# Softmax over rows on one Trainium2 core: all transfers in SyncE's queue, and the scaling by one broadcasting multiplication per group on GpSimd and VectorE

## The chip, the cores and the metric

The kernel runs on one core of a Trainium2 chip. The core has VectorE (DVE in the profile), ScalarE (ACT), GpSimd (POOL), SyncE (SP), TensorE (PE, not used here) and 16 DMA engines between the main memory and the on-chip memory, whose 128 partitions each hold a row of the tile at work. The metric is the time of one execution on the device, in microseconds (us), as a median over runs.

## The reference

The input is 16 x 1024 rows of 512 float32 numbers; each row is turned into its softmax.

```python
def reference(x: np.ndarray) -> np.ndarray:   # x: (16, 1024, 512) float32
    x_max = np.max(x, axis=-1, keepdims=True)
    exp_x = np.exp(x - x_max)
    return (exp_x / np.sum(exp_x, axis=-1, keepdims=True)).astype(np.float32)
```

## The kernel before, in words

The 16,384 rows are cut into eight chunks of 2,048 rows. In a chunk every partition holds 16 consecutive rows, so that one chunk is one transfer of 4 MB, 32 KB for each partition. The tile `held` has six places for chunks; chunk k lies in place k modulo 6, and all the work is done in place: a row is loaded, overwritten by its exponentials, overwritten again by the scaled result, and stored from there. Chunks 6 and 7 go into places 0 and 1, so their loads have to wait until the stores of chunks 0 and 1 have landed.

A chunk is worked on in two groups of eight rows per partition (`GROUP`), which makes sixteen groups, numbered 0 to 15; groups 2k and 2k+1 belong to chunk k. Each group takes three steps:

- `rowmax(g)`, line 88: one VectorE instruction takes the negated maximum of each of the eight rows and writes them to `shift`.
- `exps(g)`, line 93: eight ScalarE instructions, one for each row, compute the exponentials with `shift` as the bias, and leave the row's sum in `sums`.
- `scale(g)`: a VectorE reciprocal of the eight sums (line 104, into `recip`) and then eight VectorE instructions (line 106), one for each row, that multiply the row by its reciprocal.

The schedule is written out by hand (`tc.manual_schedule`), and every engine takes its instructions in program order. The loop over the groups calls `rowmax(g)`, `exps(g)` and then `scale(g - 1)`, so VectorE does the maximum of a group before it scales the group in front.

The six loads at the start are issued from SyncE's queue (line 71), the first one ahead of the start barrier (`loads_at_the_head`). The eight stores are issued from ScalarE's queue (line 74), among its exponentials. `STORE_BEHIND` says how many groups later than the last group of its chunk a store is placed, and `LOAD_AFTER` places the loads of chunks 6 and 7 in SyncE's queue at the points of the program at which the stores of chunks 0 and 1 are placed in ScalarE's. The small tiles `shift`, `sums` and `recip` have six buffers each.

Of the kernel before, what the change touches and what calls it, by code (L numbers as in the profile page):

```python
# [1 line left out]

# [4 lines left out]

F32 = mybir.dt.float32
EXP = mybir.ActivationFunctionType.Exp
AX = mybir.AxisListType.X  # L10


CHUNK = 16
CHUNKS = 8
PLACES = 6
GROUP = 8

STORE_BEHIND = [1, 1, 1, 1, 0, 0, 0, 0]

LOAD_AFTER = {0: 6, 1: 7}  # L20


AT_HEAD = {mybir.EngineType.SP: 1}

def loads_at_the_head(nc):

    main, body = nc.main_func.blocks[0], nc.main_func.blocks[1]
    for engine, count in AT_HEAD.items():  # L30
        loads = [
            i
            for i in body.instructions
            if i.engine == engine and type(i).__name__ == "InstDMACopy"
        ][:count]
        barrier = next(
            n
            for n, i in enumerate(main.instructions)
            if i.engine == engine and type(i).__name__ == "InstDrain"
        )  # L40
        for load in loads:
            body.instructions.remove(load)
        main.instructions[barrier:barrier] = loads


@with_exitstack
def kernel(
    ctx: ExitStack,
    tc: tile.TileContext,
    x: bass.AP,  # L50
    out: bass.AP,
):
    nc = tc.nc
    nc.at_finalize(loads_at_the_head)
    P = nc.NUM_PARTITIONS

    x_rows = x.flatten_outer_dims().rearrange("(c p r) d -> c p r d", p=P, r=CHUNK)
    out_rows = out.flatten_outer_dims().rearrange("(c p r) d -> c p r d", p=P, r=CHUNK)
    n, _, _, d = x_rows.shape
    assert n == CHUNKS  # L60

    data = ctx.enter_context(tc.tile_pool(name="data", bufs=1))
    stats = ctx.enter_context(tc.tile_pool(name="stats", bufs=6))
    held = data.tile([P, PLACES * CHUNK, d], F32, name="held")

    def place(k):
        at = (k % PLACES) * CHUNK
        return held[:, at : at + CHUNK, :]

    def load(k):  # L70
        nc.sync.dma_start(out=place(k), in_=x_rows[k])  # L71

    def store(k):
        nc.scalar.dma_start(out=out_rows[k], in_=place(k))
        if k in LOAD_AFTER:
            load(LOAD_AFTER[k])

    per = CHUNK // GROUP
    groups = CHUNKS * per
    shift, sums = [None] * groups, [None] * groups  # L80

    def rows(g):
        at = (g % per) * GROUP
        return place(g // per)[:, at : at + GROUP, :]

    def rowmax(g):
        shift[g] = stats.tile([P, GROUP], F32, name="shift", tag="shift")
        nc.vector.reduce_max(out=shift[g], in_=rows(g), axis=AX, negate=True)  # L88

    def exps(g):  # L90
        sums[g] = stats.tile([P, GROUP], F32, name="sums", tag="sums")
        for r in range(GROUP):
            nc.scalar.activation(  # L93
                out=rows(g)[:, r, :],
                in_=rows(g)[:, r, :],
                func=EXP,
                bias=shift[g][:, r : r + 1],
                scale=1.0,
                accum_out=sums[g][:, r : r + 1],
            )  # L100

    def scale(g):
        recip = stats.tile([P, GROUP], F32, name="recip", tag="recip")
        nc.vector.reciprocal(out=recip, in_=sums[g])  # L104
        for r in range(GROUP):
            nc.vector.tensor_scalar_mul(  # L106
                out=rows(g)[:, r, :],
                in0=rows(g)[:, r, :],
                scalar1=recip[:, r : r + 1],
            )  # L110

    with tc.manual_schedule():
        for k in range(PLACES):
            load(k)
        stored = 0
        for g in range(groups):
            rowmax(g)
            exps(g)
            if g:
                scale(g - 1)  # L120
            if stored < CHUNKS and g > (stored + 1) * per - 1 + STORE_BEHIND[stored]:
                store(stored)
                stored += 1
        scale(groups - 1)
        while stored < CHUNKS:
            store(stored)
            stored += 1


# [1 line left out]
_INS = ['x']  # L131
_OUTS = [((16, 1024, 512), 'float32')]


# [23 lines left out]
```

## Time and profile before

| | |
|---|---|
| Median of 3 runs (lowest to highest) | 161.43 us (161.29 to 161.83) |
| The profiled execution: its own time, and its span | 161.69 us, 159.9 us |
| VectorE busy | 123.5 us, 77% of the span |
| ScalarE busy | 93.2 us, 58% of the span |
| GpSimd busy | 0.2 us |
| Read from and written to main memory | 33.55 MB each, 420 GB/s in the mean |
| Packets of the loads' and of the stores' DMA queue | 49.5% and 48.6% of the time of 16 DMA engines |

The profile is that of one execution. The span is the time from the first to the last instruction or transfer; the execution's own time is 1.8 us longer. The share of a DMA queue is the time that its packets took, over the time of all 16 engines. In a group of instructions "busy, mean ns of one" is the sum and the mean of the instructions' durations; successive instructions of VectorE or ScalarE can overlap by their ends, so the distance from one start to the next can be shorter than the mean.

### The profile page before, as it was taken

The numbers are of one execution on the slowest core, as the hardware profiler recorded it, in microseconds if no ns is written. First come the engines' busy times: TensorE is split into PE (matmuls) and PEld (weight loads), VectorE is DVE, ScalarE is ACT, GpSimd is POOL, SyncE is SP. The second block draws the span as 40 slices with busy tenths as digits, with TensorE's granted clock in tenths as the row PEclk, the third lists the DMA queues.
The fourth block names the chain that finished last, engine by engine and source line by source line (L and its number), as shares of the span: only waits on it lengthen the run. The fifth ranks groups of instructions, "written<-read, shape, count | busy, mean of one in ns | idle before, by whom it ended". The sixth has DMA issues, their size and how long they took to land.

```text
span 159.9 us, 496 instructions
## 1 busy us (share of the span) xinstructions
DVE 123.5 (77%) x160; ACT 93.2 (58%) x257; POOL 0.2 (0%) x4
## 2 busy tenths in 40 slices
DVE  0008969999999999999999999999999997620000
ACT  0003799495959585867777685959594959300000
POOL 0000000000000000000000000000000000000000
DMA  8999999999999999999999999999999999999993
GB/s 270 459 443 402 451 459 402 426 469 410 402 393 393 500 412 402 467 434 410 426 459 410 418 484 404 402 500 410 402 426 484 393 410 500 402 402 500 410 402 148
DMA packets 2307, 67.13 MB, mean 420 GB/s; under 512 B 256, under 2 KB 256, under 8 KB 256
## 3 DMA queue, kind: packets, MB, share of 16 engines
q1 hardware_dynamic: 1152, 33.55, 49.5%
q10 hardware_dynamic: 1152, 33.55, 48.6%
q14 instruction: 3, 0.02, 0.0%
HBM read 33.55 MB, written 33.55 MB: 420 GB/s over the span
## 4 chain that ended last, share of the span: by engine, by line
DMA 48%; DVE 32%; ACT 8%; issue 1%; DVEq 0%; SPq 0%; ACTq 0%
DMA held<-in_x_dram 30%; DVE shift L88 19%; DMA out_dram<-held 18%; DVE held L106 12%; ACT held L93 8%; DVE recip L104 1%; DVEq L153 0%; SPq L71 0%; ACTq L93 0%
## 5 line engine op out<-in xcount | busy, mean ns | idle before, releaser
L93 ACT ACTIVATE held<-held,shift 128x512 f32<-128x512 f32 x128 | 90.5, 708 | 31.5 <-DVE shift L88 21.3
L88 DVE TENSOR_REDUCE shift<-held 128x8 f32<-128x4096 f32 x16 | 70.5, 4415 | 12.7 <-DMA held<-in_x_dram 12.7
L106 DVE TENSOR_SCALAR held<-held,recip 128x512 f32<-128x512 f32 x128 | 52.1, 482 | 0.6
L93 ACT ACTIVATION_READ_ACCUMULATOR held<-held,shift 128x1 f32 x128 | 23.9, 187 | 0.0
L93 ACT ACT_TABLE_LOAD x1 | 1.3, 1283 | 12.6 <-DMA held<-in_x_dram 12.6
L104 DVE RECIPROCAL recip<-sums 128x8 f32<-128x8 f32 x16 | 3.1, 196 | 4.0 <-ACT held L93 4.0
L142 POOL MEMSET const-bfloat16-1.0<- 128x1 bf16 x1 | 0.1, 101 | 0.0
L142 POOL MEMSET const-uint8-127<- 128x1 uint8 x1 | 0.1, 101 | 0.0
L142 POOL MEMSET const-float32-0.0<- 128x1 f32 x1 | 0.1, 98 | 0.2 <-issue 0.2
L142 POOL MEMSET const-float32-1.0<- 128x1 f32 x1 | 0.1, 98 | 0.0
## 6 DMA issues: line engine op xcount, KB each, us to landing
held<-in_x_dram SPq DMA_DIRECT2D x8, 4096.0 KB, 35.4
out_dram<-held ACTq DMA_DIRECT2D x8, 4096.0 KB, 28.4
```

Source lines behind the costliest of these rows:

```text
L88: nc.vector.reduce_max(out=shift[g], in_=rows(g), axis=AX, negate=True)
L93: nc.scalar.activation(out=rows(g)[:, r, :], in_=rows(g)[:, r, :], func=EXP, bias=shift[g][:, r : r + 1], scale=1.0, accum_out=sums[g][:, ...
L104: nc.vector.reciprocal(out=recip, in_=sums[g])
L106: nc.vector.tensor_scalar_mul(out=rows(g)[:, r, :], in0=rows(g)[:, r, :], scalar1=recip[:, r : r + 1],)
L142: nc = _bacc.Bacc("TRN2", target_bir_lowering=False, num_devices=1)
```

## The change

All stores are issued from SyncE's queue as well, so the order of the sixteen transfers is that of one queue: loads 0 to 5, store 0, store 1, load 6, store 2, load 7, then stores 3 to 7. A store now stands directly behind the scaling of the second group of its chunk (`finish`), and `STORE_BEHIND` is gone.

The eight multiplications of a group become one instruction over 128 x 4096 numbers, whose second operand is `recip`, repeated along each row. For groups 0 to 11 GpSimd issues it, for groups 12 to 15 VectorE. The reciprocal stays on VectorE, as do the maxima.

```diff
-STORE_BEHIND = [1, 1, 1, 1, 0, 0, 0, 0]
+LOAD_BEHIND = {1: 6, 2: 7}

-LOAD_AFTER = {0: 6, 1: 7}
+ON_POOL = range(12)
...
     def store(k):
-        nc.scalar.dma_start(out=out_rows[k], in_=place(k))
-        if k in LOAD_AFTER:
-            load(LOAD_AFTER[k])
+        nc.sync.dma_start(out=out_rows[k], in_=place(k))
+        if k in LOAD_BEHIND:
+            load(LOAD_BEHIND[k])
...
     def scale(g):
         recip = stats.tile([P, GROUP], F32, name="recip", tag="recip")
         nc.vector.reciprocal(out=recip, in_=sums[g])
-        for r in range(GROUP):
-            nc.vector.tensor_scalar_mul(
-                out=rows(g)[:, r, :],
-                in0=rows(g)[:, r, :],
-                scalar1=recip[:, r : r + 1],
-            )
+        engine = nc.gpsimd if g in ON_POOL else nc.vector
+        engine.tensor_mul(
+            out=rows(g),
+            in0=rows(g),
+            in1=recip.unsqueeze(2).to_broadcast([P, GROUP, d]),
+        )
+
+    def finish(g):
+        scale(g)
+        if (g + 1) % per == 0:
+            store(g // per)
...
-        stored = 0
         for g in range(groups):
             rowmax(g)
             exps(g)
             if g:
-                scale(g - 1)
-            if stored < CHUNKS and g > (stored + 1) * per - 1 + STORE_BEHIND[stored]:
-                store(stored)
-                stored += 1
-        scale(groups - 1)
-        while stored < CHUNKS:
-            store(stored)
-            stored += 1
+                finish(g - 1)
+        finish(groups - 1)
```

## The prediction

> **What bounds the kernel now.** I read the page's head and its 40 slices first, then the DMA queues, the busy time by stage, the groups of instructions, and the timeline around the first scaling.
>
> ```profile
> span 159.9 us, 496 instructions
> DVE 123.5 (77%) x160; ACT 93.2 (58%) x257; POOL 0.2 (0%) x4
> DMA  8999999999999999999999999999999999999993
> q1 hardware_dynamic: 1152, 33.55, 49.5%
> q10 hardware_dynamic: 1152, 33.55, 48.6%
> ```
>
> The DMA engines are full from the first slice to the last, and the two queues share them half and half (q1 loads, q10 stores). No compute engine comes near. The stages say the same:
>
> ```profile
> 12.50:40.00 27.50, 25.90 (x27) 20.09 (x54) 0.00 (x0) 1.00 1.01 435
> 56.00:84.00 28.00, 27.89 (x34) 20.79 (x59) 0.00 (x0) 1.00 1.00 431
> 84.00:120.00 36.00, 35.62 (x51) 27.29 (x77) 0.00 (x0) 1.00 1.00 432
> 141.00:160.00 19.00, 0.00 (x0) 0.00 (x0) 0.00 (x0) 1.00 0.84 364
> ```
>
> The last two columns are the DMA share and the rate. Loads alone (12.5 to 40), both directions (56 to 120): 431 to 435 GB/s throughout. One queue fills the engines as well as two do, so the single queue by itself neither costs nor brings rate. The trace's records of single packets put the loads' landings at 12.5, 22.2, 31.9 and 41.6 us: 9.69 us for a transfer that has the engines to itself, and the last four stores are as far apart. The first packet starts 1.34 us after the first issue, the last ends at 159.1, 0.8 before the end of the span. So sixteen transfers end to end, the first landing at 12.5, would end at 12.5 + 15 x 9.69 = 157.9, the span at 158.7. Before is only 1.2 us above that. The gain has a floor at that; the loss has none.
>
> The time is the span plus 1.79 us for the profiled execution (161.69 - 159.9), and that execution lies 0.26 above the median of the runs; so I add 1.53 to a span. Full engines give 158.7 + 1.53 = 160.2.
>
> **The transfers.** In one queue the slots begin, if nothing is late: store 0 at 60.9, store 1 at 70.6, load 6 at 80.3 (landing 90.0), store 2 at 90.0, load 7 at 99.7 (landing 109.4), stores 3 to 7 at 109.4, 119.1, 128.8, 138.5 and 148.2. Load 6 waits in SyncE's queue until store 0 has landed (70.6), under cover of store 1's 9.69 us; load 7 waits for store 1 (80.3), under cover of load 6 and store 2. Behind each wait stand all later transfers: a store that isn't ready stops even those that are. That is the price of the fixed order. ScalarE is rid of eight issues of some 0.34 us and SyncE gets eight, with 9.7 us for each: nothing. A store's issue must come 1.34 us before its slot (the first load's latency). So group 5 must be scaled by 88.7, group 7 by 108.1, group 9 by 117.8, group 11 by 127.5.
>
> **The compute that stays.**
>
> ```profile
> L93 ACT ACTIVATE held<-held,shift 128x512 f32<-128x512 f32 x128 | 90.5, 708 | 31.5 <-DVE shift L88 21.3
> L88 DVE TENSOR_REDUCE shift<-held 128x8 f32<-128x4096 f32 x16 | 70.5, 4415 | 12.7 <-DMA held<-in_x_dram 12.7
> L106 DVE TENSOR_SCALAR held<-held,recip 128x512 f32<-128x512 f32 x128 | 52.1, 482 | 0.6
> L142 POOL MEMSET const-bfloat16-1.0<- 128x1 bf16 x1 | 0.1, 101 | 0.0
> ```
>
> ```profile
> 22.74 0.20 DVE L104 RECIPROCAL recip<-sums 128x8 f32<-128x8 f32 x1 [1.49 <-ACT held L93]
> 22.98 3.26 DVE L106 TENSOR_SCALAR held<-held,recip 128x512 f32<-128x512 f32 x8
> 26.15 4.42 DVE L88 TENSOR_REDUCE shift<-held 128x8 f32<-128x4096 f32 x1
> ```
>
> A group now costs VectorE 4.42 + 0.2 + 3.26 = 7.9 us in a row. The change takes 3.26 of that away for twelve groups, and ScalarE, which waited 21.3 us for `shift`, then sets the pace with 5.76 us for eight exponentials (16.96 to 22.71 in the chain of waits). Off the path: group 11 is exponentiated by 86, and its scaling is due at 127.5.
>
> **The multiplications on GpSimd.** Group 0 can start at 23.0, and twelve of them run one behind the other, since GpSimd will be slower than ScalarE's 5.76. The trace has nothing of GpSimd but fills of 0.1 us, so the price P of 128 x 4096 products is bounded by VectorE's rows. Below: 4.42, the maximum's pass over one operand of that size. Above: 13.2, three such passes one after the other (two operands read, one written). I take two passes, 8.83, because the instruction reads two operands and nothing shows that GpSimd can read them side by side. Without any disturbance group 9 is then done at 23.0 + 88.3 = 111.3, in time, and group 11 at 129.0, 1.5 us late. P = 8.70 would be just in time. At 13.2 group 11 is done at 181.4, and the time is 181.4 + 1.34 + 3 x 9.69 + 0.8 + 1.53 = 214.
>
> **The multiplications on VectorE.** Four passes of 128 x 4096; bounds 3.26 (the present eight instructions) and 8.83 (two passes); I take 4.42, one pass, as the maximum's row of the same size. Alone they are hidden: group 15 is scaled by about 133, and due at 146.9. But they run while GpSimd works off its backlog, on two operands each, as it does. What they cost each other lies between nothing and full exclusion. The row that bears on it is L106: 512 products start every 407 ns, while the maximum passes 512 numbers in 4415/8 = 552. VectorE thus reads one tensor faster than one stream does, so it has a second way into memory, which a second operand would use. Whether GpSimd uses that same way, no row shows. I take exclusion, instruction by instruction, as likelier, since it needs only that the second operand of the one and the operands of the other meet at that one way; no cost stays in the range.
>
> The Trainium skill ("SBUF — State Buffer", section "Who interferes with whom") speaks against the change here: a VectorE instruction with two operands in the on-chip memory and a GpSimd instruction that reads it exclude each other for a whole instruction, and VectorE's plain reduction excludes nobody. By that rule the time is the 174.9 below, without it 161.7; nothing of before shows it.
>
> The walk, with taking turns: maximum 12 from 90.0, exponentials to 100.2; VectorE asks for multiplication 12 at 100.5, gets it when GpSimd ends group 8 (102.5), to 106.9. GpSimd does group 9 to 115.7. Load 7 lands at 109.4, maximum 14 to 113.8, multiplication 13 asked for at 114.0, run 115.7 to 120.1. Group 10 to 128.9. Multiplication 14, asked for at 124.8, 128.9 to 133.3. Group 11 from 133.3 to 142.2. GpSimd loses three turns, 3 x 4.42 = 13.2. Store 5 starts at 143.5 instead of 128.8; with stores 6 and 7 behind it the last packet ends at 143.5 + 29.1 = 172.6, the span at 173.4, the time is 174.9.
>
> For P a page has a figure ("GPSIMD Engine Reference", section "Elementwise — side-by-side cycle accounting"): 4497 ns for 2048 float32 sums per partition. Doubled, an estimate of 8.99 us for ours; the same walk would give 176.8. No row here shows it.
>
> **The rivals.**
>
> Taking turns (forecast): 174.9. If GpSimd is never made to wait and VectorE is, multiplication 12 starts at 129.0, and VectorE's four multiplications and two maxima in a row, with exponentials 15 between, end at 157.2; store 7 then ends at 168.2 and the time is 170.5. Sharing in part lies between 162 and 175. For it: both engines read two operands, and GpSimd has work in every moment at which VectorE asks. Against it: no row.
>
> GpSimd late by itself, no disturbance: 158.7 + 1.5 + 1.53 = 161.7 at P = 8.83, 163.8 at P = 9.0, 160.2 at 8.70. Most of it is no change or a little slower.
>
> No stall at all, the faster side: the engines stay full, 160.2; and 160.9 if the slow packets that before has at 40 to 44 us, as its first store starts, come again (0.66 us). It decides at P = 8.70 without disturbance and at (127.5 - 23.0 - 13.2)/12 = 7.6 with three lost turns. For it: P could be as low as 4.42, and the disturbance unreal.
>
> GpSimd much slower, P over 9.2: upwards of 177 with taking turns, up to 214 without.
>
> That the change doesn't do what it says I give nothing: in the built program the sixteen transfers stand in SyncE's queue in the order named, and the twelve multiplications in GpSimd's.
>
> **How the numbers follow.** Exclusion in whole or in part 0.45; late without disturbance 0.22 (faster 0.02, no change 0.10, slower 0.10); no stall 0.24; much slower 0.09. A measurement of this kernel can tell a change from none at about 0.3%, 0.5 us. So faster 0.26, same 0.10, slower 0.64. The predicted time is the first case's, 174.9; its own range is 166 to 177. The range must reach down to the no-stall case and leaves out the much slower one: 160.0 to 177.0.
>
> **What would show it right or wrong.** Right: GpSimd's twelve multiplications end near 142, three of them or the gaps before them stretched by some 4.4 us in 100 to 135; the DMA row falls to zero from about 129 to 143; SyncE's longest wait stands before store 5. Wrong in price: a GpSimd row far from 8.8 us. Wrong in exclusion: VectorE's multiplications at 4.4 us beside an unbroken row of GpSimd's. Wrong altogether: a DMA row of nines to the end, a span of 158.7, and the last transfer store 7 at 148.2.

## The result and the profile after

The changed kernel takes 163.65 us (163.43 to 163.99), the kernel before 161.63 us in the same comparison: a ratio of 1.0119, 95% interval 1.0093 to 1.0145. It is slower, by 2.0 us, and not by the 13 that were forecast.

The first view is the head of the changed kernel's page: busy time of the engines, the 40 slices, the rate in each slice, and the DMA queues.

```profile
span 161.4 us, 412 instructions
DVE 92.7 (57%) x36; ACT 91.9 (57%) x257; POOL 83.9 (52%) x16
POOL 0000039999999999999999999940000000000000
DMA  7999999999999999999989999999999999999990
GB/s 268 487 414 398 487 414 398 489 406 406 487 406 406 479 292 463 439 390 471 439 384 479 431 390 471 439 390 463 447 390 463 447 390 463 447 390 463 447 390 16
q1 hardware_dynamic: 2304, 67.11, 97.4%
q14 instruction: 2, 0.02, 0.0%
```

The DMA row is full to the end: the hole that was forecast for 129 to 143 us isn't there. GpSimd is done by slice 27, at 106.5 us, 21 us before its last group was due. What has changed is the last slice. It is 4 us long and moves 16 GB/s, which is two packets of 32 KB; in the kernel before the last slice moved 148 GB/s. For its last two microseconds the span waits for one DMA engine of sixteen. Of the kernel before, the rates and the queue that the prediction does not show:

```profile
GB/s 270 459 443 402 451 459 402 426 469 410 402 393 393 500 412 402 467 434 410 426 459 410 418 484 404 402 500 410 402 426 484 393 410 500 402 402 500 410 402 148
q14 instruction: 3, 0.02, 0.0%
```

The groups of instructions, and VectorE's timeline where its first multiplication meets GpSimd's last:

```profile
L93 ACT ACTIVATE held<-held,shift 128x512 f32<-128x512 f32 x128 | 90.3, 707 | 27.1 <-DVE recip L104 24.0
L106 POOL TENSOR_TENSOR held<-held,recip 128x4096 f32<-128x4096 f32 x12 | 83.7, 7022 | 22.3 <-DVE recip L104 22.3
L88 DVE TENSOR_REDUCE shift<-held 128x8 f32<-128x4096 f32 x16 | 70.1, 4388 | 27.3 <-DMA held<-in_x_dram 27.3
L106 DVE TENSOR_TENSOR held<-held,recip 128x4096 f32<-128x4096 f32 x4 | 20.6, 5139 | 0.1
```

```profile
92.51 14.00 POOL L106 TENSOR_TENSOR held<-held,recip 128x4096 f32<-128x4096 f32 x2
...
103.51 7.28 DVE L106 TENSOR_TENSOR held<-held,recip 128x4096 f32<-128x4096 f32 x1
...
116.74 4.42 DVE L106 TENSOR_TENSOR held<-held,recip 128x4096 f32<-128x4096 f32 x1
```

GpSimd's multiplication takes 7.02 us, and twelve of them follow one another without a gap. VectorE's takes 4.42 alone, and 7.28 where it began at 103.51 beside GpSimd's last, which ended at 106.51: it waited the 3.0 us and then ran its own 4.3. GpSimd was not held up at all.

The last engine can be told from the records of single packets. Every transfer ends with one completion record from each of the sixteen DMA engines. The records don't name the engine; its packets were put together by their times, since each begins where the one before it ends. The times of packets given below are 0.34 us later than the records have them, so that they match the landings. The table says how far the last and the second-to-last completion lie behind the middle one, for the last store:

```
               middle ends at   second-to-last   last
kernel before      157.85           +1.18       +1.26 us
changed kernel     157.99           +0.33       +2.55 us
```

The sum's 157.9 for sixteen transfers in a row holds for the middle engine in both. By the records every engine moves eight of a transfer's 128 packets, 128 data packets of 1.213 us in all, one behind the other and without gaps. It is late only by what is put among its packets or lengthens them. On the late engine of the changed kernel there are two 8 KB packets of the queue called "instruction" (0.31 us each, and the data packet behind each is 0.25 to 0.32 longer), and three data packets of loads that are 0.3 to 0.8 longer, at 58.8, 60.8 and 90.0 us, each the last or the last but one packet of a load with a store behind it. At 58 to 60 every engine loses time in this way (0.92 us in the middle, 1.61 on this one); at 90 only this one does (0.34).

So of the 1.88 us between the two profiled executions (163.57 and 161.69), 1.3 is the last engine's delay (2.55 - 1.26), 0.15 the middle one's, and 0.4 lies outside the span (2.17 against 1.79).

### The profile page after: what moved, and what is told of

It reads as the page before. It is cut to its first block, busy times and chain, and to the rows that moved or that the text cites. A ratio compares the mean times of both kernels' runs of the same rounds, so it can differ in the third digit from the quotient of the medians.

```text
span 161.4 us, 412 instructions
## 1 busy us (share of the span) xinstructions
DVE 92.7 (57%) x36; ACT 91.9 (57%) x257; POOL 83.9 (52%) x16
## 4 chain that ended last, share of the span: by engine, by line
DMA 46%; POOL 14%; DVE 10%; issue 8%; ACT 7%; ACTq 0%; DVEq 0%
DMA held<-in_x_dram 26%; DMA out_dram<-held 20%; POOL held L106 14%; ACT held L93 7%; DVE held L106 5%; DVE shift L88 4%; DVE recip L104 1%; ACTq L151 0%; DVEq L104 0%
## 5 line engine op out<-in xcount | busy, mean ns | idle before, releaser
L106 POOL TENSOR_TENSOR held<-held,recip 128x4096 f32<-128x4096 f32 x12 | 83.7, 7022 | 22.3 <-DVE recip L104 22.3
L106 DVE TENSOR_TENSOR held<-held,recip 128x4096 f32<-128x4096 f32 x4 | 20.6, 5139 | 0.1
```

The lines of the kernel that those rows point to most:

```text
L106: engine.tensor_mul(out=rows(g), in0=rows(g), in1=recip.unsqueeze(2).to_broadcast([P, GROUP, d]),)
```

## The experiments

All ratios are to the kernel before, on the same chip. For the profiled execution of a run, "behind" is the distance of the last engine from the middle one. A "fetch" is an 8 KB packet of the queue called "instruction", a "ring" is what one queue has waiting at one DMA engine, and a "turn" is a place where the transfers change from a load to a store.

**The queue alone, and the scaling alone.**

```diff
# e1_queue_only, against the changed kernel
-        engine = nc.gpsimd if g in ON_POOL else nc.vector
-        engine.tensor_mul(out=rows(g), in0=rows(g), in1=...)
+        for r in range(GROUP):
+            nc.vector.tensor_scalar_mul(...)        # as before
# e2_scale_only, against the kernel before
-        for r in range(GROUP):
-            nc.vector.tensor_scalar_mul(...)
+        engine = nc.gpsimd if g in ON_POOL else nc.vector
+        engine.tensor_mul(...)                      # as changed
```

> The changed kernel with the scaling of before (eight VectorE multiplications per group), so only the single queue is left of the change. Theory 'queue': in one ring each DMA engine's delays add up behind one another, and one engine (2.55 us behind the middle one at the end, by the changed kernel's packet records) ends the span; then this run is as late as the changed kernel, ratio to before 1.009 to 1.014, one engine 2 to 3 us behind. Theory 'GpSimd': the extra 2 us come from the scaling on GpSimd (instruction traffic, the time outside the span); then this run is at 0.996 to 1.003 and the last engine is at most 1.3 us behind. Theory 'fetches': VectorE's instruction stream is as long as before, so the instruction fetches fall on the same three engines as before; ratio 0.997 to 1.004.

> The kernel before with the scaling of the change (twelve groups on GpSimd, four on VectorE, one instruction each); two queues and the old order stay. Theory 'queue': ratio 0.996 to 1.003, since two rings share each engine as before. Theory 'GpSimd': ratio 1.009 to 1.014, and the time outside the span about 2.2 us instead of 1.8. Theory 'fetches': VectorE's stream is short as in the change, so the fetches that remain fall on one engine; 1.006 to 1.013, one engine 2 us or more behind.

The queue alone gave 1.0075 (1.0048 to 1.0103), the scaling alone 1.0038 (1.0006 to 1.0070). Both lie between the ranges that the theories gave; together they make 1.0113, and the whole change 1.0119. The medians of the runs tell where each acts:

```
                 span    time minus span
kernel before    160.0   1.77 us
queue alone      161.4   1.77
scaling alone    160.1   2.19
changed kernel   161.5   2.18
```

The queue lengthens the span by 1.4 us and leaves the rest alone; the scaling adds 0.4 us outside the span. Theory "queue" is right on the span in sign, and a little under its own size: e1's last engine is 1.97 behind (2 to 3 were expected), e2's 0.99. Theory "GpSimd" is right on the part outside, so far. Theory "fetches", that VectorE's shorter instruction stream moves the fetches, falls for the span: in e1 that stream is long. Two things qualify this. Two of the ten runs behind e2's ratio took 164.0 and 164.1 us, the others 161.9 to 162.5, and no profile shows the longer kind, so the scaling may now and then cost span too. And e1's engine was not late by an early fetch: the one that fetched at 34.8 us lost 0.48 us at the first store, where the middle lost 0.71, and ended with the middle. No engine was over 0.7 behind until 100 us; then the one that ends last took a fetch at 104.4 (0.60 with the packet behind it) and lost 0.87 at the end of load 7.

**No GpSimd at all** (e3).

```diff
-ON_POOL = range(12)
+ON_POOL = range(0)
```

> The changed kernel with all sixteen broadcasting multiplications on VectorE, none on GpSimd. VectorE then needs 4.4 + 0.2 + 4.4 = 9.0 us per group and ends about 12.3 + 16 x 9.0 = 157, so store 7 (due at 146.8) would be late by some 10 us if nothing else changed: span about 168, ratio 1.04. All theories expect that stall at the end; they differ in the engine spread before it: 'queue' and 'fetches' expect one engine 1.5 to 2.6 us behind at the landing of load 7, 'GpSimd' at most 1.3. The time outside the span: 'GpSimd' 1.8 us, the others 2.2.

1.060 (1.0571 to 1.0629), span 169.7, 2.03 us outside. The two lines show what a late multiplication costs in one queue:

```profile
L106 DVE TENSOR_TENSOR held<-held,recip 128x4096 f32<-128x4096 f32 x16 | 70.8, 4425 | 0.5
...
DMA  8999999999999989999999999999999942890885
```

VectorE's 8.9 us per group push the last two stores behind their slots: slices 33, 34 and 37 of the DMA row have holes. This is the kind of hole that the forecast expected of GpSimd. The expected 1.04 was too low: the expected span of 168 alone makes 1.05, and store 7 was not the only late one. Store 6 was issued at 143.0, 4 us after the middle engine had ended store 5, and store 7 at 157.8. The spread that the theories differed on, at the landing of load 7, was 1.05 us, which is "GpSimd"'s; the 2.03 outside the span is nobody's.

**Two rings with the changed order** (e4). Loads 0 to 5 go through ScalarE's queue, ahead of all its exponentials.

```diff
-AT_HEAD = {mybir.EngineType.SP: 1}
+AT_HEAD = {mybir.EngineType.Activation: 1}
...
-        nc.sync.dma_start(out=place(k), in_=x_rows[k])
+        queue = nc.scalar if k < PLACES else nc.sync
+        queue.dma_start(out=place(k), in_=x_rows[k])
```

> The changed kernel with loads 0 to 5 issued from ScalarE's queue at the start, all other transfers in SyncE's as in the change: two rings that overlap from about 37 us until load 5 has landed. Theory 'queue': the delays are shared as before, ratio 0.997 to 1.004. Theories 'GpSimd' and 'fetches': like the change, 1.009 to 1.014, one engine 2 to 3 us behind.

1.0063 (1.0038 to 1.0088): between the two expectations. The span's median is 160.6, against 161.5 in one ring; 2.19 us lie outside. The last engine is 1.12 behind, but with it six others are 0.8 us or more behind. 0.6 of the 1.5 us of span are left: here several engines share a smaller lateness, and no single one is 2 us behind.

**One turn less** (e5). Loads 6 and 7 follow each other.

```diff
-LOAD_BEHIND = {1: 6, 2: 7}
+LOAD_BEHIND = {1: (6, 7)}
...
```

> The changed kernel with loads 6 and 7 directly behind each other after store 1, so that the one queue turns from loads to stores twice (after load 5 and after load 7) instead of three times. Theory 'switch': an engine that is late when the queue turns from a load to a store pays again, 0.3 to 0.8 us at each turn; one turn less makes the last engine 0.3 us or more less late, the span 161.0 to 161.2, ratio to before 1.008 to 1.010. Theory 'fetch alone': only instruction fetches make an engine late (about 0.6 us each: 0.31 for the fetch and 0.3 for the packet behind it); the span stays at 161.5, ratio 1.011 to 1.013.

1.0091 (1.0062 to 1.0119), median span 161.3, the profiled one 161.7 with the last engine 2.93 behind: inconclusive on the time, and against the size that "switch" gave. The records show where: two fetches on that engine again (31.5 and 81.8), and at the one later turn (99.4 us) its last load packet but one is 1.00 us longer, while the load's packets on any other engine are longer by 0.14 at most. One turn less brought no gain that these runs can show.

**Fewer instructions for ScalarE** (e7). One activation per group, without the maximum; the row sums by VectorE.

```diff
-            rowmax(g)
-            exps(g)            # eight activations with bias and accum_out
+            exps(g)            # nc.scalar.activation(out=rows(g), in_=rows(g), func=EXP)
+            rowsum(g)          # nc.vector.reduce_sum(out=sums[g], in_=rows(g), axis=AX)
```

> The changed kernel without the maximum: ScalarE takes the exponentials of a whole group in one instruction without a bias, VectorE sums the rows by one reduction per group; softmax in exact arithmetic, but without the guard against overflow. ScalarE's stream falls from 128 activations to 16, VectorE's stays short, so no instruction should be fetched after the start. Transfers, queue and GpSimd's part stay. Theory 'switch' and theory 'fetch alone': without a fetch no engine is late when the queue first turns; all sixteen end within 0.5 us of the middle, span 158.9 to 159.4, time 161.1 to 161.6, ratio 0.996 to 0.999. If the single queue makes an engine late by itself, one engine is still 1 us or more behind and the ratio is over 1.003.

0.9976 (0.9958 to 0.9995): faster than the changed kernel, and just faster than the one before, in one queue, with GpSimd's twelve multiplications. The span is 159.6, 0.2 more than the expected range. Lines of this run's page, among them its DMA row and rates, and then the stretches at the end, of the changed kernel and of this one (columns: stretch, busy time of VectorE, ScalarE and GpSimd, clock, DMA share, GB/s):

```profile
L97 POOL TENSOR_TENSOR held<-held,recip 128x4096 f32<-128x4096 f32 x12 | 83.7, 7018 | 24.5 <-DVE recip L95 24.5
...
DMA  7999999999999999999999999999999999999994
GB/s 263 443 476 394 411 493 411 394 484 435 394 443 476 394 394 394 427 452 435 394 452 468 394 419 452 443 394 443 419 443 427 427 452 427 427 435 435 435 427 189
q1 hardware_dynamic: 2304, 67.11, 98.5%
```

```profile
157.00:158.00 1.00, 0.00 (x0) 0.00 (x0) 0.00 (x0) 1.00 0.08 33
158.00:159.00 1.00, 0.00 (x0) 0.00 (x0) 0.00 (x0) 1.00 0.08 33
```

```profile
157.00:158.00 1.00, 0.00 (x0) 0.00 (x0) 0.00 (x0) 1.00 0.38 164
158.00:159.00 1.00, 0.00 (x0) 0.00 (x0) 0.00 (x0) 1.00 0.00 0
```

In the changed kernel one packet per microsecond is moved at the end, by one engine; here several engines end together, the last 0.46 us behind the middle. There is no "instruction" queue in this run's list of queues: nothing was fetched during the span. So one ring makes no engine late by itself. The edit takes out more than instructions, though: the maximum is gone, and the exponentials of a group take ScalarE 3.61 us instead of 5.76. And 1.77 us lie outside the span although GpSimd multiplies, so GpSimd's work is not what adds the 0.4.

**Half the instructions** (e6). The maximum stays; each activation takes two rows, with the first one's maximum, and the scaling follows in pairs. The output is thus not the softmax of each row.

```diff
-        for r in range(GROUP):
-            nc.scalar.activation(out=rows(g)[:, r, :], ..., bias=shift[g][:, r : r + 1], accum_out=sums[g][:, r : r + 1])
+        for r in range(GROUP // 2):
+            nc.scalar.activation(out=pairs(g)[:, r, :], ..., bias=shift[g][:, 2 * r : 2 * r + 1], accum_out=sums[g][:, r : r + 1])
...
```

> The changed kernel with four activations of 1024 numbers per group instead of eight of 512 (rows are normalised in pairs, so the output is not the reference's): 64 activations instead of 128, the maximum kept, everything else as in the change. Theory 'ScalarE's stream': the late engine comes from the fetches of ScalarE's instructions; with half the stream at most one is left, the last engine is 0.5 to 1.6 us behind the middle, span 159.6 to 160.6. Rival: in the run without the maximum it was something else that cured it (VectorE's or the order's doing); then two fetches or an engine 2 us or more behind remain, span 161.2 to 161.8.

1.0055 (1.0028 to 1.0082), median span 160.45, as theory "ScalarE's stream" had it: with the maximum kept, half the activations give back about half of the 2 us. But the spans spread from 159.6 to 161.8, and the profiled one is at the upper end: a single fetch, at 50.8 us, and yet the engine that had it ends 2.93 behind, which the theory had at 1.6 at most. The fetch and the packet behind it cost 0.69. The rest was lost at the turns: 1.34 at the first store (0.86 in the middle engine), 0.95 at 89.1 and 0.68 at 109.5 (up to 0.3 on others). No execution with a short span was profiled, so what its engines do is not shown.

**Engines made late on purpose.** One more packet of 32 KB on each of three engines, in one queue (e10) and in two (e11).

```diff
         for k in range(PLACES):
             load(k)
+            if k == 1:
+                nc.sync.dma_start(out=place(5)[0:3], in_=x_rows[5][0:3])
```

> The changed kernel with one more transfer after load 1: three partitions of chunk 5, 32 KB each, which is one packet of 1.21 us on each of three DMA engines (load 5 writes the same data again, so the output is the same). These three are then 1.2 us late from 23 us on. Theory 'switch': they pay 0.8 us again at the first turn and some 0.3 at each later one, and end 2.3 us or more behind the middle; if one of them also takes ScalarE's fetches it ends 3.5 or more behind. Theory 'fetch alone': they end 1.2 us behind, and the span stays at 161.5 unless one of them is the fetching engine (then 162.7).

> The kernel before with the same three late engines (one packet more on each of three engines after load 1). Both theories: with two rings open side by side there is no turn to pay at except where the first store starts; the three engines end 1.2 to 1.9 us behind the middle, the span is 160.0 to 160.6, ratio 1.000 to 1.004. If they end 2.3 us or more behind, being late costs as much with two queues, and 'switch' falls.

1.0200 (1.0174 to 1.0227) and 1.0201 (1.0160 to 1.0242). In one queue three engines end 3.7 to 4.3 behind the middle. But they were about 3 us late already at 25 us, not 1.2, since the small transfer cost them far more than its packet (data packets beside it took up to 1.8 us longer), so the end is no test of the expectation. At the later turns they lost another 0.4 to 0.6 each, apart from the two fetches that one of them had, and the middle engine 0.02: "fetch alone" has no such term. In two queues the middle engine itself ended 1.1 us later, at 158.98, and the last three 2.0, 2.0 and 3.1 behind that; the data packets at the ends of the loads (62, 82 and 102 us) were long there too. Only one of them is over the 2.3 that was set, and that one had two fetches, so whether "switch" falls is not decided. What the two runs do show is that late engines are not cheaper in two queues: the small transfer added about 3 us to the kernel before and 1.3 to the changed one.

**Two queues with few instructions.** The kernel without the maximum, first with the queues and the order of before (e8), then without stores in ScalarE's queue (e12, with the edit of the run with loads 0 to 5 in ScalarE's queue).

> The kernel without the maximum (one activation per group, row sums by VectorE) with the two queues and the transfers' order of before. Theory 'ScalarE's stream': without fetches one and two queues tie; span 159.3 to 159.9, last engine within 0.6 us, ratio 0.996 to 0.999 like the one-queue version at 0.9976. Rival 'two queues are better anyway': ratio 0.993 or less.

> The one-queue kernel without the maximum (one activation per group, row sums by VectorE; ratio 0.9976, span 159.6), with loads 0 to 5 issued from ScalarE's queue and the rest from SyncE's, so that no store stands in ScalarE's way. Theory 'late engine': the single queue costs only because the engine that fetches instructions pays at the turns; with no fetch one and two queues tie, span 159.2 to 160.0, ratio 0.995 to 1.000. Rival 'the queue by itself': two queues are 0.8 us or more faster here as well (as 160.6 stands to 161.5 with the long instruction stream), span 158.9 or less, ratio 0.993 or less.

The first gave 1.1009 (1.0993 to 1.1024) and says nothing about rings. ScalarE stood still behind its own stores:

```profile
ACT held L89 <- POOL held L99: 63.9, 6, 15.6
```

A store in ScalarE's queue waits there for GpSimd's multiplication, and the next exponentials wait behind it. The second gave 1.0075 (1.0051 to 1.0100), span 161.45: slower than its one-queue twin by 1.6 us going by the ratios, where a tie or a gain was expected, so both expectations missed. No engine is late (0.45 behind), but the middle one ends at 159.13 instead of 158.32: it loses more around the first store (1.10 us until 70 us against 0.68) and afterwards (0.51 against 0.32). The profiled execution is among the shortest of this run (span 160.4), so the rest of the 1.6 us was not seen. Two rings are therefore not better in themselves; with no late engine, one ring was.

**A single GpSimd multiplication** at the start of the kernel before (e9).

```diff
+        nc.gpsimd.memset(spare, 1.0)
+        nc.gpsimd.tensor_mul(out=spare, in0=spare, in1=spare)
```

> The kernel before with one GpSimd multiplication of 128 x 8 on a tile of its own at the start. Outside the span lie 1.77 us in the kernel before and 2.19 in the changed one. If the mere presence of a GpSimd multiplication sets that, this run has 2.1 to 2.2 us outside its span; if not, 1.7 to 1.8 (the run without the maximum, with GpSimd at work, had 1.77, which speaks for the second).

161.96 us in its one run, 1.76 us outside the span. So neither GpSimd's presence (here) nor its work (in the run without the maximum) sets the part outside. It was 2.2 in every run that had eight or four activations per group together with the short VectorE stream and GpSimd, 2.03 in the run with VectorE alone, and 1.8 wherever either VectorE's stream was long or ScalarE's was sixteen activations. What these have in common was not found.

## Why the prediction was wrong

**The transfers.** Right: sixteen transfers in a row fill the engines; the middle engine ends at 157.99 where 157.9 was worked out. That closeness is in part luck: the sum began at 12.5, where the last engine of load 0 landed (the middle one landed at 11.96 in the changed kernel), and left out the 0.92 us that the middle engine loses at the first store. Every store was issued well before its slot, the last at 136.2 for a slot at 148.2:

```profile
L74 SPq DMA_DIRECT2D out_dram<-held x8: 332/338/717, 36.8 to 136.2; - x8
```

The lead of 1.34 us that an issue was given is 0.99 by the profile's own packet records; nothing turned on it. Wrong: the single queue "by itself neither costs nor brings rate" was a term put at nothing, and the queue alone made the span 1.4 us longer (e1). Wrong too: the sum let all engines end together. The end of the span is that of the last engine, and the kernel before's profile showed it: its end lay 1.2 us above the sum, which was read as room for a gain and was the lateness of its own last engine (1.26).

**The multiplications on GpSimd.** This is the step that failed first: P was taken as two passes of VectorE's maximum, 8.83, and measured 7.02. The price that decides was put at 8.70 without disturbance and at 7.6 with three lost turns; 7.02 is below both. GpSimd ended at 106.5 instead of 142.2, and with it the forecast's 14.7 us stall is gone. The bounds (4.42 and 13.2) held it; the price taken from "two operands, two passes" was 1.8 us too high. Whether GpSimd reads its two operands side by side the runs don't show. The figure of the Trainium skill ("GPSIMD Engine Reference", section "Elementwise — side-by-side cycle accounting"), 8.99 as an estimate, was further off than the row's.

**The multiplications on VectorE.** 4.42 was right to the digit. Half of the exclusion is shown: the one multiplication that met GpSimd's waited out its rest. This is what the Trainium skill ("SBUF — State Buffer", section "Who interferes with whom") says, and 7.28 beside 4.42 shows it in this case. In seven other runs one VectorE multiplication met GpSimd's last in the same way, and each ended 4.3 us after it; the longest, in e7, began at 103.34 and took 9.60 us, with GpSimd's last ending at 108.66. The other half is the one that the 174.9 rests on, that GpSimd in its turn waits for VectorE and loses three turns. No run shows it, since no GpSimd multiplication ever stood behind the one that VectorE met. In the changed kernel only one of the four met it, and VectorE waited under cover: store 6 was due long after.

**The rivals.** "No stall at all" had the right mechanism, a DMA row of nines to the end and store 7 as the last transfer, and the wrong price: 160.2 against 163.65. The missing 3.4 us are 2.7 of span (161.4 against 158.7: the last engine, 2.55 behind, and 0.1 for the rest), 0.4 outside it, and 0.3 from the correction to the median, which was -0.26 for the profile of before and is +0.08 here. It was given 0.24, and counted wholly on the faster side; with the price measured it lies on the slower one.

**The range and the sign.** 163.65 lies inside 160.0 to 177.0, and slower was the likelier sign. Both are luck: the reasons given for slower, a late or a hindered GpSimd, did not occur.

**What stays open.** That an engine which has fetched is late, and loses time again where a load ends, is seen in the records of the changed kernel, e5 and e6 (1.2 to 1.6 us at the first store, where the middle lost 0.7 to 0.9), and in e1 at its last turn. It is not a rule: in e1 the early fetch left no late engine, and in e3, with a fetch at 35.9 us, no engine was over 0.42 behind after the first store. Taking the instructions away took the late engine away (e7), together with other things. So fetches as the cause are likely, not proved. Why an engine loses time at a turn was only seen, not explained, and the size varies between 0.3 and 1.0 us from one later turn to the next. Why the two queues of before lose so little with three fetches, and what the 0.4 us outside the span are, stays open.

## What to carry to other kernels

In a kernel bound by DMA, look at the last engine and not at the mean: a DMA row of nines hides that one engine of sixteen may be microseconds behind (2.55 here), and the rate in the last slice shows it. Instructions can cost DMA time as well: the kernel before, with 496 instructions, had three fetches among its data packets, the changed one (412) two, e6 (286) one and e7 (166) none. The run with sixteen activations instead of 128 gave back all that the change had lost, though it also leaves out the maximum. And where a price that decides lies between two bounds three times apart, with the threshold in between, the likeliest case should not be the one that needs it on a given side.

## What the runs showed of the hardware that was not expected

- GpSimd multiplied 128 x 4096 float32 numbers by a broadcast operand in 7.01 to 7.03 us, 1.6 times VectorE's 4.42, in all nine runs that gave it this work. VectorE's maxima beside it, and a VectorE multiplication that began after it, did not lengthen it.
- The DMA engines lose time once, on the packets around the first store: 0.71 us in the middle engine of the kernel before (at 43 us), 0.92 in the changed one (at 59). In e10 and e11 a loss of 0.5 us stood at 22 us, around the small transfer of three partitions, and at the first store it was 0.04: it may belong to the first transfer that differs from those before it, which no run tested by itself.
- A transfer over three partitions of 32 KB cost its engines about 3 us each, two and a half times its packet.
